# Placement order, weight transposes, index yields and the update of x in a PEER decoder kernel

## The chip, the cores and the metric

One core of a Trainium2 chip runs the whole program in one launch. The metric is the device time of one execution in microseconds; the kernel before has a median of 2251.29 us over 3 runs. The engines are TensorE (PE, with its weight loads shown as PEld), VectorE (DVE), ScalarE (ACT), GpSimd (POOL) and SyncE (SP), which here issues the transfers.

## The reference

A decoder trunk of two layers over 256 tokens of width 1024. In each layer a mixer stage (HGRN2 and stick-breaking attention) is followed by a PEER feed-forward, which is where the change lies:

```python
q = (h @ w_pq).reshape(B, S, 8, 2, 64)
s1, s2 = q[..., 0, :] @ sub_keys[0].T, q[..., 1, :] @ sub_keys[1].T
v1, i1 = lax.top_k(s1, 16); v2, i2 = lax.top_k(s2, 16)
cand = v1[..., :, None] + v2[..., None, :]
top, pos = lax.top_k(cand, 16)
idx = take(i1 * 128 + i2, pos); gates = softmax(top)
act = gelu(einsum(h, peer_u[idx]))
out = einsum(gates * act, peer_v[idx])
```

There are 8 heads, 16384 experts and 256 tokens. After it follows a layer norm of `ALPHA * x + y`, with y scaled by a gate row.

## The kernel before, in words

The kernel doesn't gather experts. It computes all 16384 of them densely, as 128 tiles of 128 experts (`NK`), and multiplies the result by a dense map of gates that is zero where an expert isn't chosen.

**Up stage.** `u_tile` takes a tile j of `peer_u` (128 experts x 1024), turned so that the width lies on partitions and split into a high part and a low part of fp32r, and makes three products with the two parts of h over eight chunks: 24 matmuls of 128x256. Two tiles share a PSUM bank; `fin_u` then applies Gelu on ACT, and multiplies by the gates of the tokens that are already placed (L1618, DVE).

A tile passes through a chain made ahead by `take` and `prep`: transfers from HBM (four on SP's queue), a transpose, a copy that rounds to the high part (ACT, L58), and a subtraction that gives the low part (POOL, L271). Tiles are of two kinds, set by `uv_seq` (L124): kind `u` is turned by one DVE transpose of 128x1024 (`turn`, L220); kind `x`, every fourth tile, by eight PE transposes into PSUM (`prep`, L251), from which ACT copies twice per half, once as the high part and once back into the raw tile. The two kinds are loaded with different layouts. In the down stage a tile j of `peer_v` needs no turning; its low parts come from DVE (L271), and the activations are split by ACT and DVE (`split2`, L521).

**Side work.** Beside the up stage runs a generator, `select`: `topk` finds the candidates and does the index work, and `place_gates` writes the map of gates, in 64 blocks of 4 tokens. `build` compares indices with a ramp on DVE (L1499) and multiplies by the gates (L1504); `prod` makes eight small matmuls of the two into PSUM; `put` brings the result into the map: where tiles are already computed, DVE multiplies them by it (L1531), elsewhere ACT copies it. `pull` deals this work out between tiles: each tile adds a budget to a credit (kept to at most twice the budget), the generator runs on while the credit is above zero, each `yield` takes its number from the credit, and `yield None` ends the turn:

```python
for i, (kind, j) in enumerate(uv_seq[:nu]):
    u_tile(j)
    pull(sides, 1.55 + 1.2 * (kind == "x"))
```

`nu` is 126. What is left of the side work then is drained before PSUM is given to the down stage.

The order on each engine is the order in which the program issues instructions; an engine waits on semaphores for what its operands need.

**Down stage.** The 128 tiles of `peer_v` go into four PSUM banks with 12 matmuls of 128x512 each. Meanwhile the weight and bias rows of the layer norm before are loaded by POOL's queue (`load_row`, issued at step j = 32) into `g_row` and `b_row`, which lie in a buffer whose earlier contents are the gated activations of tiles 12 to 19, and POOL scales and shifts x by them at steps 38 and 44 (lines 1725 to 1728). In layer 1 both rows are loaded again at step 64.

Of the kernel before, what the change touches and what calls it, by code (L numbers as in the profile page):

```python
# [24 lines left out]
NK = 128  # L25
# [16 lines left out]
NB_J = 32  # L42
# [3 lines left out]
def trunk_kernel(ctx: ExitStack, tc: tile.TileContext, x, c, w_ada, b_ada, w_in, lb_logits, hg_norm_g,  # L46
                 w_up_a, w_up_b, w_o, w_pq, sub_keys, peer_u, peer_v, ln_g, ln_b, out):
    nc = tc.nc
# [72 lines left out]
            order.append((kind, w[l][k * P:(k + 1) * P, :], 0))  # L121


    uv_seq = [("x" if j % 4 == 3 else "u", j) for j in range(NK)] + [("v", j) for j in range(NK)]  # L124
    for l in range(DEPTH):
        if l == 0:

# [1191 lines left out]
    def peer(l, hT):  # L1319
        with ExitStack() as es:  # L1320
# [10 lines left out]
            progress = {"j": 0, "t": 0}  # L1331
            with ExitStack() as eu:
# [26 lines left out]
                def topk():  # L1359
# [89 lines left out]
                    for tt in range(2):  # L1449

                        puf = pu[tt].rearrange("p h k -> p (h k)").bitcast(U32)
                        for a in range(2):
                            nc.vector.tensor_scalar(sel[a].bitcast(U32), puf, 4 - 2 * a, None,
                                                    op0=OP.logical_shift_right)
                            nc.vector.tensor_copy(half[2 + a], iu[a][tt].rearrange("p h k -> p (h k)").bitcast(U32))

                        nc.vector.scalar_tensor_tensor(half[0], sel[1].bitcast(U32), -12.0, sel[0].bitcast(U32),
                                                       op0=OP.add, op1=OP.max)
                        for a in range(2):
                            nc.vector.scalar_tensor_tensor(sel[a], half[0], -16.0 + 12 * a, puf, op0=OP.mult, op1=OP.add)  # L1460
                        nc.vector.scalar_tensor_tensor(half[1], sel[1], -48.0, sel[0], op0=OP.add, op1=OP.max)
                        tp = top[tt]
                        yield 0.9
                        for a in range(2):
                            nc.vector.tensor_tensor(m, per_head(half[a])[:, :, :, None].to_broadcast(k4),
                                                    iota_k[:, None, None].to_broadcast(k4), op=OP.is_equal)
                            yield 1.4
                            nc.vector.tensor_mul(m, m, per_head(half[2 + a])[:, :, None].to_broadcast(k4))
                            yield 1.1
                            nc.vector.tensor_reduce(per_head(sel[a]), m, axis=mybir.AxisListType.X, op=OP.add)  # L1470
                            yield 1.4
                        nc.vector.tensor_reduce(sm[:, :PH], tp, axis=mybir.AxisListType.X, op=OP.add)
                        nc.vector.reciprocal(sm[:, :PH], sm[:, :PH])
                        nc.vector.tensor_mul(tp, tp, sm[:, :PH][:, :, None].to_broadcast([P, PH, TOPK]))
                        yield 0.8
                        yield None
                        ptr = psk.tile([P, 512], F32, name="K")
                        for q, src in enumerate((sel[0], sel[1], tp.rearrange("p h k -> p (h k)"))):
                            nc.tensor.transpose(ptr[:, q * P:(q + 1) * P], src, ident)
                        yield None  # L1480
                        nc.vector.tensor_copy(iT[:, tt * P // TB:(tt + 1) * P // TB].rearrange("p b a t -> p a b t"),
                                              ptr[:, :2 * P].rearrange("p (a b t) -> p a b t", a=2, t=TB))

                        nc.vector.tensor_scalar(rest, ptr[:, 2 * P:3 * P], GSCALE, None, op0=OP.mult)
                        pv = rest.rearrange("p (u v) -> p u v", v=2)
                        gp = gT[:, tt * P // 2:(tt + 1) * P // 2]
                        nc.vector.tensor_copy(gp[:, :, 0], pv)
                        nc.vector.tensor_sub(gp[:, :, 1], pv, gp[:, :, 0])
                        yield 0.8
                    yield None  # L1490

                def place_gates():
# [18 lines left out]
                    def prod(b):  # L1511
                        pg = psk.tile([P, TB, NK], F32, name="G")
                        o, og = built.pop(b)
                        for q in range(TB):
                            for a in range(2):
                                mm(pg[:, q], o[:, 0, q // 2, :, q % 2], og[:, q // 2, a, :, q % 2], a == 0, a == 1)
                        return pg

                    def put(b, pg):
# [11 lines left out]
                            nc.vector.tensor_mul(dst, src, dst)  # L1531
                        progress["t"] = (b + 1) * TB

                    built, prods = {}, {}
                    nb = S // TB
                    for b in range(nb + 1):
                        if 0 <= b - 1 < nb:
                            prods[b - 1] = prod(b - 1)
                        if b < nb:
                            build(b)  # L1540
                        yield 1.2
                        if 0 <= b - 1 < nb:
                            put(b - 1, prods.pop(b - 1))

                        yield 0.2 + 0.7 * progress["j"] / NK
                        yield None

                def select():
# [161 lines left out]
                for kind, j in uv_seq[nu:]:  # L1710
                    if kind != "v":
                        u_tile(j)
                        continue
                    state["ahead"] = j < NK - 1
                    delayed.append((j, *take("v"), *wsplit.popleft()))
                    v_prod(0, *delayed[-1])
                    while len(delayed) > max(0, (j - NK + LAST + 1) // 3):
                        v_prod(1, *delayed.popleft())
                    if pend:
                        fin_u(*pend.pop())  # L1720
                    if j == NB_J or l == DEPTH - 1 and j == 2 * NB_J:
                        load_row(g_row, ln_g[l, j // NB_J - 1])
                        load_row(b_row, ln_b[l, j // NB_J - 1])

                    if j in (NB_J + 6, NB_J + 12):
                        xb = from_blocks(xt[j // 6 - (NB_J + 6) // 6])
                        nc.gpsimd.tensor_mul(xb, xb, in_blocks(g_row))
                        nc.gpsimd.tensor_add(xb, xb, in_blocks(b_row))
                    mod_step(mods_left)
                    pull(sides, 0.75)  # L1730
                    if j == NK - 4:
                        drain(sides)
                        row(gt_row, l, GT2, 1.0 / GSCALE)
                        warm_sqrt()
                        if l + 1 < DEPTH:
                            A, B = fold(l, 1, l + 1, SH1, SC1)
                            hT = Modulated()
                            fulls = deque(r[:, i * S:(i + 1) * S] for r in (g_row, b_row) for i in range(4))
# [46 lines left out]
```

## Time and profile before

| | |
|---|---|
| median of 3 runs | 2251.29 us (2247.49 to 2252.64) |
| profiled execution | 2254.38 us |
| its span | 2252.6 us |
| mean granted clock | 0.982 |
| PE busy | 2135.2 us (95%) |
| PE weight loads busy | 1945.4 us (86%) |
| DVE busy | 1817.2 us (81%) |
| ACT busy | 1172.5 us (52%) |
| POOL busy | 1041.5 us (46%) |
| chain that ended last | PE 73%, DVE 16%, DMA 4%, issue 3%, ACT 3% |

All rows are of the profiled execution. A busy PE is not PE at its peak, since matmuls overlap and their ends are modelled; start-to-start distances show its pace. Idle time of an engine matters only where another waits for it. The clock is TensorE's granted clock as a share of full speed.

### The profile page before, as it was taken

Reading aid. Unit: us, or ns where it says so; the run is one execution under the profiler, and the core shown is the slowest. Engines: PE = TensorE matmul, PEld = TensorE weight load, DVE = VectorE, ACT = ScalarE, POOL = GpSimd, SP = SyncE. Lnnn points to the kernel's source line nnn. Section 1 sums busy time; section 2 is a strip of 40 time slices with the busy share of each in tenths; the row PEclk is TensorE's granted clock in tenths of the full one; section 3 lists DMA queues with packets and bytes.
Section 4 is the critical chain, followed back from the end, with each engine's and each line's share of the span. In section 5 each row is a group of like instructions: output and inputs, shape, how many; then the busy total and the mean of one; then the engine's idle time right before and its main releaser. Section 6 shows DMA issues by size and latency. Waiting matters only on the chain.

```text
span 2252.6 us, 42211 instructions
## 1 busy us (share of the span) xinstructions
PE 2135.2 (95%) x14596; PEld 1945.4 (86%) x14596; DVE 1817.2 (81%) x3278; ACT 1172.5 (52%) x2445; POOL 1041.5 (46%) x760
## 2 busy tenths in 40 slices
PE   5789899899999999999989998998999999999998
PEld 5789799899999978888779897997999999788886
DVE  7887989999997488888887558999999955666675
ACT  3446555455555545555545564554555555455562
POOL 4656637787778510000045534577777783200001
PEclk8999999999999999999999999999999999999999
DMA  8646567666667678888844335675766676666662
GB/s 273 196 137 221 159 140 159 129 148 148 142 147 156 176 236 275 281 286 283 298 134 150 113 121 142 147 153 118 154 142 148 146 164 187 202 196 192 193 227 90
DMA packets 498895, 400.32 MB, mean 178 GB/s; under 512 B 291920, under 2 KB 446072, under 8 KB 498680
## 3 DMA queue, kind: packets, MB, share of 16 engines
q1 hardware_dynamic: 496936, 392.33, 62.8%
q0 software_dynamic: 1408, 4.23, 0.6%
q8 instruction: 115, 1.88, 0.3%
q10 hardware_dynamic: 336, 1.06, 0.1%
q14 instruction: 100, 0.82, 0.1%
HBM read 396.46 MB, written 1.05 MB: 176 GB/s over the span
## 4 chain that ended last, share of the span: by engine, by line
PE 73%; DVE 16%; DMA 4%; issue 3%; ACT 3%; POOL 1%; SPq 1%; POOLq 0%; ACTq 0%; DVEq 0%
PE A L61 28%; PE Y L61 27%; PE T L61 7%; PE G L61 4%; PE T L251 2%; DVE wl L271 2%; PE ss L61 2%; PE hs L61 2%; DMA raw<-in_peer_u_dram 2%; POOL wl L271 1%; DVE qk L857 1%; DMA raw<-in_peer_v_dram 1%; DVE raw L220 1%; DVE e L843 1%; DVE o L1504 1%
## 5 line engine op out<-in xcount | busy, mean ns | idle before, releaser
L271 POOL TENSOR_TENSOR wl<-raw,wh 128x512 fp32r<-128x512 f32 x663 | 914.3, 1406 | 700.9 <-ACT wh L58 582.4
L58 ACT ACTIVATE wh<-raw 128x512 fp32r<-128x512 f32 x1060 | 610.8, 623 | 182.0 <-PE A L61 47.6
L61 PE MATMUL A<-hTh,wh 128*128 128x256 f32 x2080 | 543.3, 293 | 11.9 <-ACT wh L58 11.8
L61 PE MATMUL A<-hTl,wh 128*128 128x256 f32 x2080 | 524.2, 284 | 0.0
L61 PE MATMUL Y<-wh,o 128*128 128x512 f32 x1776 | 480.5, 392 | 0.8 <-DVE o L521 0.8
L271 DVE TENSOR_TENSOR wl<-raw,wh 128x512 fp32r<-128x512 f32 x525 | 380.2, 765 | 63.5 <-ACT wh L58 44.9
L61 PEld LDWEIGHTS A<-hTh,wh 128*128 128x128 f32 x2080 | 400.6, 193 | 14.4 <-ACT wh L58 13.7
L61 PEld LDWEIGHTS A<-hTl,wh 128*128 128x128 f32 x2080 | 401.7, 193 | 0.8 <-DVE hTl L521 0.2
L61 PEld LDWEIGHTS Y<-wh,o 128*128 128x128 f32 x1776 | 334.9, 189 | 70.8 <-DVE o L521 1.2
L61 PE MATMUL A<-hTh,wl 128*128 128x256 f32 x2080 | 337.9, 285 | 11.0 <-POOL wl L271 10.9
L61 PEld LDWEIGHTS A<-hTh,wl 128*128 128x128 f32 x2080 | 288.9, 193 | 14.2 <-POOL wl L271 14.2
L61 PE MATMUL Y<-wl,o 128*128 128x512 f32 x888 | 277.9, 393 | 10.4 <-DVE wl L271 10.4
L220 DVE STREAM_TRANSPOSE raw<-raw 128x1024 f32<-128x1024 f32 x192 | 235.1, 1230 | 11.7 <-DMA raw<-in_peer_u_dram 10.1
L58 ACT ACTIVATE o<-buf 128x256 fp32r<-128x256 f32 x228 | 95.1, 417 | 282.7 <-PE Y L61 282.7
L521 DVE TENSOR_TENSOR o<-buf,o 128x256 fp32r<-128x256 f32 x228 | 100.1, 439 | 150.4 <-ACT o L58 150.4
L61 PEld LDWEIGHTS Y<-wl,o 128*128 128x128 f32 x888 | 168.1, 189 | 48.9 <-DVE wl L271 13.8
L1499 DVE TENSOR_TENSOR o<-iT,iota_t 128x1024 f16<-128x1024 f16 x128 | 163.9, 1280 | 0.0
L58 ACT ACTIVATE buf<-G 128x128 f32<-128x128 f32 (+4 forms) x244 | 56.0, 276 | 203.6 <-PE G L61 203.6
L570 POOL TENSOR_TENSOR x<-x,buf 128x1024 f32<-128x1024 f32 x1 | 2.4, 2392 | 291.0 <-DVE x L567 291.0
L61 PE MATMUL T<-hTh,wh 128*128 128x256 f32 x512 | 133.6, 293 | 0.0
L61 PE MATMUL T<-hTl,wh 128*128 128x256 f32 x512 | 130.1, 286 | 0.0
L1504 DVE TENSOR_TENSOR o<-gT,o 128x1024 f16<-128x1024 f16 x128 | 124.6, 973 | 4.4
(496 smaller groups left out, 3254.9 us busy)
## 6 DMA issues: line engine op xcount, KB each, us to landing
raw<-in_peer_u_dram SPq DMA_DIRECT2D x1024, 128.0 KB, 3.5
raw<-in_peer_v_dram SPq DMA_DIRECT2D x256, 512.0 KB, 4.4
raw<-in_w_in_dram SPq DMA_DIRECT2D x88, 512.0 KB, 4.9
raw<-in_w_ada_dram SPq DMA_DIRECT2D x78, 512.0 KB, 4.9
raw<-in_w_o_dram SPq DMA_DIRECT2D x16, 512.0 KB, 3.5
raw<-in_w_pq_dram SPq DMA_DIRECT2D x64, 128.0 KB, 3.4
qk<-in_w_ada_dram SPq DMA_DIRECT2D x10, 512.0 KB, 3.9
e<-in_w_ada_dram SPq DMA_DIRECT2D x8, 512.0 KB, 6.0
```

What stands on the lines that cost most here:

```text
L58: nc.scalar.activation(o, i, f, **kw)
L61: nc.tensor.matmul(o, a, b, start=start, stop=stop, **kw)
L220: nc.vector.transpose(t, t)
L251: nc.tensor.transpose(banks[s][:, q], t[:, (4 * s + q) * P:(4 * s + q + 1) * P], ident)
L271: eng.tensor_sub(lo, src, h.bitcast(F32))
L521: nc.vector.tensor_sub(lo, src, h.bitcast(F32))
L570: nc.gpsimd.tensor_mul(xt[tt], xt[tt], last[0])
L843: eng.tensor_sub(ev[:, :, :hn], mid, bv[:, :, :hn])
L857: nc.vector.tensor_mul(tv[:, :, hn:], nodes(qT, n)[:, :, hn:], ev[:, :, hn:])
L1499: nc.vector.tensor_tensor(o.rearrange("p a u n v -> p (a u) n v"), iT[:, b].rearrange("p a (u v) -> p (a u) v", v=2)[:, :, None] .to_broad ...
L1504: nc.vector.tensor_mul(og.rearrange("p u a n v -> p (u a) n v"), gT[:, b * nu:(b + 1) * nu].rearrange("p u a v -> p (u a) v")[:, :, None] ...
```

## The change

Four edits. Every fourth tile is of kind `x` in the first 64 tiles only; the others from there on become kind `u`, and the budget of their turn falls from 2.75 to 1.55 with the kind. The index work yields after each small instruction, and the charges of the large ones rise. In `place_gates` a turn is now: put block b-2, build block b, issue the matmuls of block b-1 (before: matmuls of b-1, build b, put b-1). And x is scaled and shifted in 16 operations over a quarter of 256 columns, issued at steps 38 to 53, one a step, not in four over 1024.

```diff
-    uv_seq = [("x" if j % 4 == 3 else "u", j) for j in range(NK)] + ...
+    uv_seq = [("x" if j % 4 == 3 and j < NK // 2 else "u", j) for j in range(NK)] + ...
...
                             nc.vector.tensor_scalar(sel[a].bitcast(U32), puf, 4 - 2 * a, None,
                                                     op0=OP.logical_shift_right)
+                            yield 0.5
                             nc.vector.tensor_copy(half[2 + a], iu[a][tt].rearrange("p h k -> p (h k)").bitcast(U32))
+                            yield 0.6
...
                         nc.vector.scalar_tensor_tensor(half[0], sel[1].bitcast(U32), -12.0, sel[0].bitcast(U32),
                                                        op0=OP.add, op1=OP.max)
+                        yield 0.5
                         for a in range(2):
                             nc.vector.scalar_tensor_tensor(sel[a], half[0], -16.0 + 12 * a, puf, op0=OP.mult, op1=OP.add)
+                            yield 0.5
                         nc.vector.scalar_tensor_tensor(half[1], sel[1], -48.0, sel[0], op0=OP.add, op1=OP.max)
                         tp = top[tt]
-                        yield 0.9
+                        yield 0.5
                         for a in range(2):
...
-                            yield 1.4
+                            yield 1.7
                             nc.vector.tensor_mul(m, m, per_head(half[2 + a])[:, :, None].to_broadcast(k4))
                             yield 1.1
                             nc.vector.tensor_reduce(per_head(sel[a]), m, axis=mybir.AxisListType.X, op=OP.add)
-                            yield 1.4
+                            yield 1.6
...
-                    for b in range(nb + 1):
-                        if 0 <= b - 1 < nb:
-                            prods[b - 1] = prod(b - 1)
+                    for b in range(nb + 2):
+                        if b >= 2:
+                            put(b - 2, prods.pop(b - 2))
+
+                            yield 0.2 + 0.7 * progress["j"] / NK
                         if b < nb:
                             build(b)
-                        yield 1.2
-                        if 0 <= b - 1 < nb:
-                            put(b - 1, prods.pop(b - 1))
-
-                        yield 0.2 + 0.7 * progress["j"] / NK
+                            yield 1.2
+                        if 1 <= b <= nb:
+                            prods[b - 1] = prod(b - 1)
                         yield None
...
-                    if j in (NB_J + 6, NB_J + 12):
-                        xb = from_blocks(xt[j // 6 - (NB_J + 6) // 6])
-                        nc.gpsimd.tensor_mul(xb, xb, in_blocks(g_row))
-                        nc.gpsimd.tensor_add(xb, xb, in_blocks(b_row))
+                    n = j - NB_J - 6
+                    if 0 <= n < 16:
+                        xb = from_blocks(xt[n // 8])[:, n % 4]
+                        (nc.gpsimd.tensor_add if n // 4 % 2 else nc.gpsimd.tensor_mul)(
+                            xb, xb, in_blocks(b_row if n // 4 % 2 else g_row)[:, n % 4])
```

## Rows read from the trace of the kernel before

**Rows 1.** the page, busy tenths in 40 slices of 56.3 us, VectorE

```profile
DVE  7887989999997488888887558999999955666675
```

**Rows 2.** busy by stage: stretch, length, PE, PEld, DVE, ACT, POOL (instructions), clock, DMA

```profile
412.00:471.00 59.00, 49.79 (x373) 47.54 (x373) 56.83 (x69) 26.02 (x47) 46.30 (x31) 0.94 0.58 123
471.00:705.00 234.00, 233.22 (x2176) 228.20 (x2175) 229.83 (x335) 129.67 (x342) 180.87 (x129) 1.00 0.66 148
705.00:768.00 63.00, 62.97 (x533) 62.77 (x533) 28.47 (x34) 34.58 (x64) 52.18 (x42) 1.00 0.76 169
1517.00:1576.00 59.00, 47.94 (x356) 45.58 (x355) 57.54 (x67) 25.12 (x45) 41.58 (x29) 0.94 0.58 118
```

**Rows 3.** waits, index stretch 412 to 471 us: total us, times, longest

```profile
PEld A L61 <- POOL wl L271: 7.1, 8, 1.5
```

**Rows 4.** timeline of DVE in the index stretch: start, duration in us

```profile
417.17 0.22 DVE L1453 TENSOR_SCALAR buf<-buf 128x128 uint32<-128x128 uint32 x1
...
420.86 1.23 DVE L220 STREAM_TRANSPOSE raw<-raw 128x1024 f32<-128x1024 f32 x1
```

**Rows 5.** timeline of PE at a tile turned on PE, in the tail

```profile
757.31 0.64 PE L61 MATMUL A<-hTh,wl 128*128 128x256 f32 x4
757.79 1.04 PE L251 MATMUL T<-ident,raw 128*128 128x128 f32 x8
758.58 0.36 PE L61 MATMUL A<-hTh,wh 128*128 128x256 f32 x1
```

**Rows 6.** groups of DVE in the placement stretch, 471 to 705 us

```profile
L1499 DVE TENSOR_TENSOR o<-iT,iota_t 128x1024 f16<-128x1024 f16 x63 | 81.1, 1288 | 0.0
L1504 DVE TENSOR_TENSOR o<-gT,o 128x1024 f16<-128x1024 f16 x63 | 60.7, 963 | 2.2
L220 DVE STREAM_TRANSPOSE raw<-raw 128x1024 f32<-128x1024 f32 x48 | 59.1, 1232 | 0.0
L1531 DVE TENSOR_TENSOR buf<-G,buf 128x128 f32<-128x128 f32 (+19 forms) x129 | 31.9, 289 | 0.0
L1618 DVE TENSOR_TENSOR buf<-A,buf 128x8 f32<-128x8 f32 (+31 forms) x32 | 12.9, 404 | 2.0 <-ACT A L58 1.4
```

**Rows 7.** waits in the placement stretch, 471 to 705 us

```profile
ACT buf L58 <- PE G L61: 99.5, 63, 2.9
...
PEld L61 <- DVE o L1504: 3.6, 14, 0.3
```

**Rows 8.** busy by stage, down stage: x updated in layer 0, undisturbed, layer 1

```profile
826.00:850.00 24.00, 18.38 (x64) 13.95 (x63) 21.43 (x20) 7.96 (x17) 10.46 (x5) 0.86 0.65 215
900.00:925.00 25.00, 25.00 (x114) 20.68 (x113) 21.09 (x36) 12.85 (x27) 0.00 (x0) 1.00 0.84 275
1930.00:1956.00 26.00, 21.26 (x80) 16.44 (x79) 19.34 (x21) 9.74 (x20) 11.59 (x7) 0.87 0.64 202
```

**Rows 9.** timelines of POOL, then DVE, while x is updated in layer 0

```profile
828.91 2.37 POOL L1727 TENSOR_TENSOR x<-x,buf 128x1024 f32<-128x1024 f32 x1
834.82 2.37 POOL L1728 TENSOR_TENSOR x<-x,buf 128x1024 f32<-128x1024 f32 x1 [3.55 <-DMA buf<-in_ln_b_dram]
837.15 2.58 POOL L1727 TENSOR_TENSOR x<-x,buf 128x1024 f32<-128x1024 f32 x1
...
837.40 5.62 DVE L271 TENSOR_TENSOR wl<-raw,wh 128x512 fp32r<-128x512 f32 x2
842.94 0.41 DVE L521 TENSOR_TENSOR o<-buf,o 128x256 fp32r<-128x256 f32 x1
843.28 1.28 DVE L271 TENSOR_TENSOR wl<-raw,wh 128x512 fp32r<-128x512 f32 x2
```

**Rows 10.** instructions of the tile raw: duration ns min/median/max, first and last start

```profile
L271 POOL TENSOR_TENSOR wl<-raw,wh x663: 1260/1302/2957, 19.1 to 1879.6; 128x512 fp32r<-128x512 f32 x166
```

**Rows 11.** instructions of lines 1499 and 1504, the same columns

```profile
L1499 DVE TENSOR_TENSOR o<-iT,iota_t x128: 644/1324/1780, 470.6 to 1811.6; 128x1024 f16<-128x1024 f16 x128
...
L1504 DVE TENSOR_TENSOR o<-gT,o x128: 691/692/1779, 471.3 to 1812.3; 128x1024 f16<-128x1024 f16 x128
```

More of the change, by code (lines that the diff above doesn't have):

```diff
@@ L121, in add_rows @@
             order.append((kind, w[l][k * P:(k + 1) * P, :], 0))
-    uv_seq = [("x" if j % 4 == 3 else "u", j) for j in range(NK)] + [("v", j) for j in range(NK)]
+    uv_seq = [("x" if j % 4 == 3 and j < NK // 2 else "u", j) for j in range(NK)] + [("v", j) for j in range(NK)]
     for l in range(DEPTH):
```

## The prediction, made before the changed kernel was run

> **What bounds the kernel now.** I read the page's slices first: VectorE (DVE) is at nine tenths or more in the 7th to 12th and 26th to 32nd slice, the expert-up stage of the two layers [rows 1]. So the next view is busy time by stage. In layer 0 the up stage falls into three stretches [rows 2]: index work (412 to 471 us), where TensorE (PE) is busy 49.8 of 59 us and its clock averages 0.94; placement (471 to 705), where PE has 233.2 and DVE 229.8 of 234 us, so both are full; and a tail (705 to 768) after the last placement, where PE is full and DVE busy only 28.5 of 63. Layer 1 has the same stretches. Three facts follow. PE loses time in the index work; placement is bound by two engines at once; DVE has some 34 us of air at the end, which comes too late to be used.
>
> The waits in the index stretch say who is late there: weight loads and matmuls wait for the low halves from GpSimd (POOL) [rows 3], which wait for the conversion, which waits for the DVE transpose of a tile. The timeline shows why: seven index operations issued as one lump hold DVE from 417.17 to 420.86, and the tile's transpose starts only then [rows 4].
>
> **Index yields (before lines 1452 to 1471).** Work is dealt out by credit: a tile brings 1.55 (2.75 if its weights are turned on PE), work runs while credit is above zero, each yield charges, and a bare yield ends the turn. Charged per half of the tokens: 0.9 + 2 x 3.9 + 0.8 + 0.8 = 10.3 before, 4.1 + 0.1 + 2 x 4.4 + 1.6 = 14.6 after. At 1.85 a tile on average, two halves take 11 tiles before and 16 after, and with the bare yields 14 and 18 (tiles 26 to 40 and 26 to 44, counting the credit tile by tile). DVE's own work doesn't change: 56.8 busy less 14 x 0.75 transposes of 1.23 [rows 6] is 44 us, and 18 tiles add 18 x 0.75 x 1.23 = 16.6, together 60 us. PE's floor for 18 tiles: 24 matmuls at 0.12 are 2.88 us, a quarter of the tiles adds 0.79 for PE transposes [rows 5], so 3.08 a tile and 55 us. I take 60 us for 18 tiles against 59 for 14: DVE stays the bound, but four more tiles pass below it. Bounds: 55 (PE's floor) to 70 (four tiles more at today's placement pace, nothing won).
>
> **Transposes in the first half only (line 124).** Placement of layer 0 holds 63 blocks and, by 48 DVE and 16 PE transposes, 64 tiles in 234 us: 3.63 us a tile [rows 2, 6]. DVE's groups add up to 245.7 us against 229.8 busy (ends overlap), so I scale by 0.935: a block costs DVE (81.1 + 60.7 + 31.9) x 0.935 / 63 = 2.58 us, a transpose 1.15, the gate product of a tile 0.19 on average and some 0.23 later on. On PE a block costs what is left: (234 - 64 x 2.88 - 16 x 0.79) / 63 = 0.59.
>
> The change takes 16 x 0.79 = 13 us from PE in each layer and puts 16 x 1.15 = 18 us on DVE; the 32 ScalarE copies per layer that go too were on an engine busy 130 of 234 us, and POOL's two subtractions and the four transfers of a tile stay. It also takes 1.2 of credit from each of those 16 tiles. From tile 64 on a tile brings 1.55, a block charges 1.4 + 0.7 j/128, about 1.9, so some 0.85 blocks go to a tile: placement ends at tile 118, not 105, and still ahead of tile 126, so nothing is left to drain with PE idle. Those 54 tiles with 46 blocks cost DVE 46 x 2.58 + 54 x 1.15 + 54 x 0.23 = 193 us, with today's 2% of idle 197; PE needs 54 x 2.88 + 46 x 0.59 = 183. **DVE becomes the bound there**, and 197 is what I take; PE's 183 is the lower bound, the upper one stands under the rivals. The last 8 tiles run at 2.88, 23 us.
>
> **Put ahead of the next comparison (lines 1536 to 1546).** In each turn ScalarE's copies of a block wait for PE's placement matmuls: 99.5 us in 63 waits [rows 7]. Putting block b-2 first makes those waits vanish, as its matmuls were issued a turn earlier. But PE waits for the block's DVE operand only 3.6 us in 234, so there is at most that to win; the block's order on PE's queue stays behind the same tile, and a second block in PSUM has its bank. On DVE the put now stands ahead of the comparison, and both need matmuls of the turn before, so no new wait is queued in front of the transposes. I take nothing, between -3.6 and, if DVE's collisions below shift, a loss priced as the second rival.
>
> **Sum of the up stage**, layer 0, tiles 26 to 126: before 14 tiles in 59, 65 at 3.63 (236), 21 at 3.08 (65), together 360, against 356 in the rows. After: 60 + 20 tiles at 3.6 (72) + 197 + 23 = 352. So -8 by the sums and -4 against the rows; I take -6, and -12 for the two layers.
>
> **x in 16 pieces (lines 1725 to 1728).** Where POOL scales x in the down stage, PE falls: 64 matmuls in 24 us and 80 in 26 at clocks of 0.86 and 0.87, where an undisturbed 25 us has 114 [rows 8]. At 4.56 a microsecond 45 and 39 are missing, 9.9 and 8.5 us, **18 us in all**. The timeline shows the cause: a POOL operation over 128x1024 takes 2.4 us, and two DVE subtractions beside two of these took 5.62 us, not 1.28 [rows 9]: each waited for one POOL operation. The diff spreads the pieces over 16 turns, but that is the order of the program, not of time: the second mul at 837.15 starts right behind the first add, though it is issued six turns (16 us) later than the first mul, and POOL is idle at 900, when nothing of it was left. POOL has nothing else queued, so the pieces will run back to back too, once the rows have landed. A 128x512 operation takes 1.26 [rows 10], one of 1024 2.37; the line through both gives 0.7 for 256 (estimate), 11.3 us for 16 against 10.1 for four. What changes is that DVE gets its turn after 0.7. Layer 1: a step's DVE work is 0.41 + 1.28 = 1.69 us [rows 9], three waits of up to 0.7 make it 3.8 against a step of 2.63 (12 of 114 matmuls in 25 us); 12 pieces in a row last some 3.5 steps and put DVE 4 us behind, of which the tile made one step ahead hides some 2.5. In layer 0 DVE has 21.1 of 25 us, 2.2 a step; with 3.5 waits it is 4.6, and 7 us behind, less 2.5. So 2 and 4 us stay lost, without the fall of the clock, against 9.9 and 8.5: about -12, of which I take **-11**. Bounds: 0 to -18.
>
> The later row loads of layer 1 stand behind the pieces on POOL's queue and start about 1 us later; they are wanted at the end of the span only.
>
> **Together** -12 - 11 = -23 on the profiled execution's 2254.4 us (span 2252.6): 2231. The runs' median stands 3 us below it, so 2229.
>
> **Rivals.**
> *PE's floor.* With ScalarE out of the way and fewer blocks a tile, DVE collides less: its two fp16 operations take 0.64 and 0.69 us undisturbed, 1.29 and 0.96 on average [rows 6, 11]. Then tiles 64 to 118 go at PE's 183 and the index work at 55: 19 us less per layer than above, -23 against the rows for each, with -11 together -57: 2194. For it: 0.9 us a block is waiting; against: POOL is as busy per tile as before. Chance 0.14.
> *DVE's pace worsens.* The same collisions, other way: the new order shifts when the comparison meets POOL's subtractions. Each can wait for a whole one (maxima 1.78 us [rows 11]). From 0.25 us more a block, 46 blocks in each layer give back the 23 us; at 0.45 more it is -23 + 41 = +18, 2269. For it: DVE has no air left before tile 118; against: the mean of both has been the same in both layers. Chance 0.11.
> *Pieces win nothing.* DVE is shut out for 11.3 us in sum, more than before; if PE loses it all, only -12 is left, 2239. Against: PE can draw on a tile made ahead. Chance 0.2. The Trainium skill, SBUF — State Buffer, section "Who interferes with whom", says that a VectorE instruction with two SBUF inputs and a GpSimd instruction that reads SBUF exclude each other for the whole instruction; by that alone cutting an operation up saves no locked time. The trace agrees on the lock with the 5.62 us, but no run here shows pieces.
> *The retuning cancels out.* The extra tiles in the index work only trade places with air, so that the up stage gives its -4 or nothing, and the pieces win little: within 4.5 us. Chance 0.1.
>
> **Numbers.** The forecast (2229, its own range 2212 to 2242) has 0.45. A measurement of this kernel can tell 0.2%, 4.5 us, from no change. Faster: 0.45 + 0.14 + 0.2 = 0.79; same 0.1; slower 0.11. The range leaves out most of the DVE rival and half of PE's floor: 2200 to 2250.
>
> **What would show it.** Last comparison near tile 118, not 105, the tail short; DVE at 98% through it with PE's weight loads waiting for the transpose chain or the block's operand; index stretch PE above 52 of 59 us; no ScalarE wait for the placement matmuls; POOL's 16 pieces within some 20 us, PE there above 90% at full clock. Wrong if L1499 and L1504 change their means by 0.2 us or more, if blocks are drained after tile 126, or if the pieces run one to a step.

## The result, and the profile after

The changed kernel takes 2276.32 us (median of 4 runs, 2276.01 to 2277.69) against 2250.96 for the kernel before: a ratio of 1.0116, 95% interval [1.0098, 1.0133]. That is 25 us slower; 22 us faster had been forecast. Three of the kernels further down (e2, e9 and e12) had one execution each of 11102, 2344 and 5303 us; their medians are those of the other executions. The profiled execution has a span of 2274.6 us, so 22.0 us more than before.

Where these 22.0 us lie shows when both traces are cut at the same events: the first 128x256 matmul of an up stage, the first and the last matmul into Y. The columns are us.

| stage | before | after | difference |
|---|---|---|---|
| up stage, layer 0 | 453.4 | 470.1 | +16.7 |
| down stage, layer 0 | 372.4 | 367.9 | -4.4 |
| mixers, layer 1, and its queries | 277.7 | 278.8 | +1.1 |
| up stage, layer 1 | 456.2 | 470.1 | +13.9 |
| down stage, layer 1, to the end | 369.5 | 363.8 | -5.7 |

The down stages gained 10.2 us, where 11 had been forecast. The up stages were to gain 12 us together and lost 31. Busy time by stage of the changed kernel in layer 0, with the columns of [rows 2]: index work, placement while every fourth tile is turned on PE, placement with all tiles turned on DVE, and the tail:

```profile
412.00:476.00 64.00, 54.98 (x441) 52.71 (x440) 62.93 (x68) 31.04 (x56) 54.08 (x36) 1.00 0.63 136
476.00:550.00 74.00, 72.51 (x670) 70.70 (x669) 69.22 (x98) 40.11 (x104) 60.07 (x41) 1.00 0.68 147
550.00:765.00 215.00, 191.16 (x1681) 181.68 (x1679) 207.91 (x278) 89.34 (x235) 169.05 (x110) 0.99 0.50 135
765.00:787.00 22.00, 22.00 (x188) 22.00 (x186) 14.09 (x19) 11.87 (x22) 20.88 (x17) 1.00 0.72 195
```

The index stretch has 403 matmuls of tiles (the other 38 are transposes), at 24 a tile some 17 tiles in 64 us or 3.8 each, where the kernel before had 14 at 4.1 [rows 2]. The next stretch goes at the old pace. The loss is in the third: 1314 of its 1681 matmuls belong to tiles (the rest are placement), 54.8 tiles in 215 us, **3.93 us a tile where 3.65 was forecast**; PE is busy 191 of 215, and DVE, the bound, 208. DVE's groups of that stretch, as [rows 6]:

```profile
L1508 DVE TENSOR_TENSOR o<-gT,o 128x1024 f16<-128x1024 f16 x46 | 76.7, 1667 | 1.6
L220 DVE STREAM_TRANSPOSE raw<-raw 128x1024 f32<-128x1024 f32 x55 | 67.1, 1227 | 0.0
L1503 DVE TENSOR_TENSOR o<-iT,iota_t 128x1024 f16<-128x1024 f16 x45 | 38.2, 849 | 0.0
```

The transposes cost 1.23 us as ever. The pair of a block, 1503 and 1508 here, 1499 and 1504 before, costs 0.85 + 1.67 = 2.52 us; it was 2.25 in the old placement stretch [rows 6]. Over the whole program each line of the pair (ns, columns as [rows 11]):

```profile
L1503 DVE TENSOR_TENSOR o<-iT,iota_t x128: 644/667/1790, 479.6 to 1879.1; 128x1024 f16<-128x1024 f16 x128
...
L1508 DVE TENSOR_TENSOR o<-gT,o x128: 691/1670/1794, 480.3 to 1879.8; 128x1024 f16<-128x1024 f16 x128
```

The medians have changed places. Before, the comparison usually waited (1324 ns, against a minimum of 644) and the product did not (692); now the comparison is free (667) and the product waits, and waits longer (1670 against 691). Of the 256 operations of the pair 150 take over 1 us in either kernel: not more of them wait, but others, and for longer. One tile of the changed kernel shows why; these are the timelines of DVE, then ACT, POOL and PE, with start and duration in us:

```profile
624.16 1.23 DVE L220 STREAM_TRANSPOSE raw<-raw 128x1024 f32<-128x1024 f32 x1
625.32 0.40 DVE L1623 TENSOR_TENSOR buf<-A,buf 128x272 f32<-128x272 f32 x1
625.65 0.54 DVE L1535 TENSOR_TENSOR buf<-G,buf 128x128 f32<-128x128 f32 x2
626.12 0.67 DVE L1503 TENSOR_TENSOR o<-iT,iota_t 128x1024 f16<-128x1024 f16 x1
626.82 1.67 DVE L1508 TENSOR_TENSOR o<-gT,o 128x1024 f16<-128x1024 f16 x1
...
625.55 1.16 ACT L58 ACTIVATE wh<-raw 128x512 fp32r<-128x512 f32 x2 [1.78 <-POOL wl L271]
...
626.26 3.37 POOL L271 TENSOR_TENSOR wl<-raw,wh 128x512 fp32r<-128x512 f32 x2 [0.87 <-ACT wh L58]
...
628.55 0.63 PE L61 MATMUL G<-o,o 128*128 128x128 f16 x8 [0.70 <-DVE o L1508]
```

The transpose ends at 625.39, and ACT's conversion of that tile starts at 625.55. In this stretch 47 of 53 conversions start within 0.2 us of the end of their transpose; in the placement of the kernel before, 1 of 48. (The profile names POOL's subtraction before as the releaser; it ends in the same moment.) POOL's next subtraction is issued at 626.26, while DVE's comparison runs (626.12 to 626.79). Both have two inputs in SBUF. If they exclude each other, which the experiments on POOL test, POOL gets in when the comparison ends, just ahead of the product, which has to wait for most of it: 1.67 us, not 0.69. PE stands idle 0.70 us for that product before its placement matmuls. The cycle then repeats in the same phase. A tile of the kernel before, DVE, ACT and POOL:

```profile
599.21 1.44 DVE L1499 TENSOR_TENSOR o<-iT,iota_t 128x1024 f16<-128x1024 f16 x1
600.68 0.69 DVE L1504 TENSOR_TENSOR o<-gT,o 128x1024 f16<-128x1024 f16 x1
601.29 0.52 DVE L1531 TENSOR_TENSOR buf<-G,buf 128x128 f32<-128x128 f32 x2
...
599.78 0.41 ACT L58 ACTIVATE buf<-G 128x88 f32<-128x88 f32 x2 [1.95 <-PE G L61]
600.08 1.15 ACT L58 ACTIVATE wh<-raw 128x512 fp32r<-128x512 f32 x2
...
600.80 2.99 POOL L271 TENSOR_TENSOR wl<-raw,wh 128x512 fp32r<-128x512 f32 x2 [0.69 <-ACT wh L58]
```

Here ACT starts with copies that wait 1.95 us for PE's placement matmuls, so the conversion comes at 600.08 and POOL's subtraction at 600.80. The comparison at 599.21 meets the rest of the subtraction before (1.44, not 0.65), and the product at 600.68 gets in ahead of the new one: 0.69. What the copies waited for was free, and it held POOL back.

In the third stretch ACT's copies no longer wait for the placement matmuls (99.5 us in [rows 7]), as forecast, but the wait of PE's weight loads for the product has grown from 3.6 us to 24.6. The waits (total us, times, longest):

```profile
ACT wh L58 <- POOL wl L271: 83.2, 33, 3.7
...
PEld L61 <- DVE o L1508: 24.6, 24, 2.2
...
PE G L61 <- DVE o L1508: 19.8, 24, 2.0
```

In the down stage PE loses less than before while x is updated, at full clock (columns as [rows 8]):

```profile
825.00:850.00 25.00, 22.45 (x99) 18.29 (x98) 20.93 (x29) 12.37 (x26) 3.92 (x6) 1.00 0.87 297
850.00:875.00 25.00, 23.46 (x103) 17.83 (x102) 24.27 (x32) 10.65 (x23) 13.76 (x12) 1.00 0.74 246
```

228 matmuls were due in 50 us at the undisturbed rate, 202 came: 26 missing, 5.7 us, where 45 had been (9.9 us). The pieces do run back to back, four and then twelve, and not one to a step; 13.76 us for twelve is 1.15 us each, as DVE takes turns with POOL there. Beside the four it gets no turn: of two DVE subtractions that take 1.28 us alone, the second starts at 845.78 and ends only after all four, 3.67 us later. That is longer than any beside the four large operations of the kernel before (3.25), and layer 1 shows the same (3.49):

```profile
845.18 4.27 DVE L271 TENSOR_TENSOR wl<-raw,wh 128x512 fp32r<-128x512 f32 x2
...
846.11 2.77 POOL L1734 TENSOR_TENSOR x<-x,buf 128x256 f32<-128x256 f32 x4
851.05 13.76 POOL L1734 TENSOR_TENSOR x<-x,buf 128x256 f32<-128x256 f32 x12 [2.17 <-DMA buf<-in_ln_b_dram]
```

### The profile page after: what moved, and what is told of

It is laid out like the page before. It is cut to its first block, busy times and chain, and to the rows that moved or that the text cites. A ratio compares the mean times of both kernels' runs of the same rounds, so it can differ in the third digit from the quotient of the medians.

```text
span 2274.6 us, 41907 instructions
## 1 busy us (share of the span) xinstructions
PE 2117.0 (93%) x14340; PEld 1917.6 (84%) x14340; DVE 1892.0 (83%) x3324; ACT 1134.0 (50%) x2371; POOL 1098.5 (48%) x784
## 4 chain that ended last, share of the span: by engine, by line
PE 55%; DVE 17%; issue 8%; POOL 8%; DMA 6%; ACT 3%; SPq 2%; POOLq 0%; DVEq 0%; ACTq 0%
PE Y L61 26%; PE A L61 15%; POOL wl L271 8%; PE T L61 6%; DMA raw<-in_peer_u_dram 4%; PE hs L61 2%; PE ss L61 2%; DVE wl L271 2%; PE G L61 2%; SPq L197 2%; DVE o L1508 1%; DVE raw L220 1%; DVE qk L857 1%; PE T L251 1%; DMA raw<-in_peer_v_dram 1%
## 5 line engine op out<-in xcount | busy, mean ns | idle before, releaser
L271 POOL TENSOR_TENSOR wl<-raw,wh 128x512 fp32r<-128x512 f32 x663 | 959.9, 1475 | 675.8 <-ACT wh L58 603.5
L58 ACT ACTIVATE wh<-raw 128x512 fp32r<-128x512 f32 x1124 | 647.6, 622 | 459.3 <-POOL wl L271 241.1
L220 DVE STREAM_TRANSPOSE raw<-raw 128x1024 f32<-128x1024 f32 x224 | 273.6, 1228 | 0.6 <-DMA raw<-in_peer_u_dram 0.5
L1508 DVE TENSOR_TENSOR o<-gT,o 128x1024 f16<-128x1024 f16 x128 | 206.6, 1614 | 4.4
L61 PE MATMUL G<-o,o 128*128 128x128 f16 x1024 | 81.4, 220 | 42.7 <-DVE o L1508 42.7
L1503 DVE TENSOR_TENSOR o<-iT,iota_t 128x1024 f16<-128x1024 f16 x128 | 111.4, 870 | 0.0
```

The source lines that it names most:

```text
L58: nc.scalar.activation(o, i, f, **kw)
L61: nc.tensor.matmul(o, a, b, start=start, stop=stop, **kw)
L220: nc.vector.transpose(t, t)
L271: eng.tensor_sub(lo, src, h.bitcast(F32))
L1503: nc.vector.tensor_tensor(o.rearrange("p a u n v -> p (a u) n v"), iT[:, b].rearrange("p a (u v) -> p (a u) v", v=2)[:, :, None] .to_broad ...
L1508: nc.vector.tensor_mul(og.rearrange("p u a n v -> p (u a) n v"), gT[:, b * nu:(b + 1) * nu].rearrange("p u a v -> p (u a) v")[:, :, None] ...
```

## The experiments

**One edit at a time.** The kernels of the experiments are called e1 to e12. Each of the first four is the kernel before with one of the four edits.

First e1, PE transposes in the first half only:

```diff
-    uv_seq = [("x" if j % 4 == 3 else "u", j) ...
+    uv_seq = [("x" if j % 4 == 3 and j < NK // 2 else "u", j) ...
```

> Kernel before with the PE transposes in the first half only, and nothing else. Theory A (the new order of placement makes the collisions between DVE and POOL; it is not in this kernel): the DVE operations of lines 1499 and 1504 stay near 2.2 us a block together, and the up stage of each layer changes by -4 to +6 us, total within 2243 to 2263. Theory B (the 16 more DVE transposes per layer are the loss by themselves, whatever the order): the up stages are 14 us or more longer each, total about 2280.

Measured: 2253.09 us, ratio 1.0005 [0.9995, 1.0015], no difference. The pair takes 1.11 + 1.17 = 2.28 us a block. Theory B falls: 16 more DVE transposes per layer cost nothing by themselves. That PE gives back as much is likely, not shown.

e2, the order of placement:

```diff
-                        if 0 <= b - 1 < nb:
-                            prods[b - 1] = prod(b - 1)
+                        if b >= 2:
+                            put(b - 2, prods.pop(b - 2))
...
                             build(b)
...
-                            put(b - 1, prods.pop(b - 1))
+                            prods[b - 1] = prod(b - 1)
```

> Kernel before with put ahead of the next comparison, and nothing else. Theory A (the order makes the collisions): L1504 (its line here) takes about 1.6 us on average where it took 0.96, the pair some 0.3 us a block more, about +15 us per layer, total about 2275 or more. Theory C (the collisions need both, the order and tiles that are all turned on DVE): the pair stays within 0.1 us of the kernel before, total within 2246 to 2256.

Measured: 2290.38 us, ratio 1.0185 [1.0164, 1.0205]: **some 40 us slower, more than the whole change**. The up stages are 18.6 and 17.3 us longer. The pair, over the whole program:

```profile
L1504 DVE TENSOR_TENSOR o<-gT,o 128x1024 f16<-128x1024 f16 x128 | 184.4, 1441 | 4.4
L1499 DVE TENSOR_TENSOR o<-iT,iota_t 128x1024 f16<-128x1024 f16 x128 | 123.3, 963 | 0.0
```

2.40 us a block against 2.25 in the kernel before (1.280 + 0.973 over its whole program): theory A, not C. The 0.15 us are 10 us over 64 blocks, though, of 18 lost. DVE also idles more: in the placement stretch its gate product (L1618, here 1619) waits 7.8 us for ACT's Gelu, 1.4 before [rows 6].

e3, the index yields:

```diff
                             nc.vector.tensor_scalar(sel[a].bitcast(U32), puf, ...
+                            yield 0.5
...
-                            yield 1.4
+                            yield 1.7
```

> Kernel before with the index yields only. By the prediction's step: four more tiles pass beside the index work for 1 to 5 us more, the tail is shorter by five tiles: -4 to -9 us per layer, total 2235 to 2245. Rival: DVE is the bound from the topk work on, so the tiles only trade places: within 2247 to 2256.

Measured: 2244.20 us, ratio 0.9972 [0.9961, 0.9982]: 7 us faster, up stages 3.7 and 5.3 us shorter. The gain is real and at the small end. The down stage of layer 0, which the edit doesn't touch, is 3.9 us shorter in that trace too.

e4, x in 16 pieces:

```diff
-                    if j in (NB_J + 6, NB_J + 12):
-                        xb = from_blocks(xt[...])
-                        nc.gpsimd.tensor_mul(xb, ...); nc.gpsimd.tensor_add(xb, ...)
+                    n = j - NB_J - 6
+                    if 0 <= n < 16:
+                        xb = from_blocks(xt[n // 8])[:, n % 4]
+                        (nc.gpsimd.tensor_add if n // 4 % 2 else nc.gpsimd.tensor_mul)(xb, xb, ...)
```

> Kernel before with x in 16 pieces only. The changed kernel's down stages were 4.4 and 5.8 us shorter than those of the kernel before: if that is the pieces alone, this kernel takes about 2241 (2238 to 2244). Rival: the down stage is shorter because of something that the other edits leave behind (a tile of peer_v made earlier), then within 2248 to 2254.

Measured: 2246.18 us, ratio 0.9975 [0.9962, 0.9988], 5 us faster (3 to 9 by the interval), between the two ranges expected. In its trace the down stages are 5.5 and 5.9 us shorter, so the pieces do it by themselves; the up stages of that one execution are 2.6 and 1.3 us longer than those of before, which the edit doesn't touch. How much is scatter shows in all fourteen traces. In layer 1 the down stage takes 368.0 to 369.5 us without the pieces and 363.7 to 363.9 with them, a plain gain of 5 us; in layer 0 it takes 368.4 to 373.1 without and 365.4 to 369.1 with them, 3 us by the means. Together that is 8 us.

**What of the order is slow.** In the next kernel, e5, put is cut in two: put itself makes ACT's copies, right behind the matmuls again, and hands back DVE's products, which stay ahead of the comparison of the following turn.

```diff
                         if b >= 2:
-                            put(b - 2, prods.pop(b - 2))
+                            for dst, src in prods.pop(b - 2):
+                                nc.vector.tensor_mul(dst, src, dst)
...
                         if 1 <= b <= nb:
-                            prods[b - 1] = prod(b - 1)
+                            prods[b - 1] = put(b - 1, prod(b - 1))
```

> The kernel of e2 (put ahead of the comparison), but put is cut in two: ScalarE's copies of block b-1 are issued right behind its matmuls, as in the kernel before, and only DVE's product of block b-2 stands ahead of the comparison. Theory A1 (ScalarE's wait for the placement matmuls, which e2 lost, kept the conversion and with it POOL's subtraction behind the end of a tile on PE, out of the way of line 1504): the pair of lines 1499 and 1504 is back at 2.2 to 2.3 us, total 2246 to 2260. Theory A2 (the place of DVE's product between the transpose and the comparison is what shifts the pair into POOL's subtraction): as slow as e2, 2280 or more.

Measured: 2270.37 us, ratio 1.0095 [1.0071, 1.0118]: between the two, so neither theory as it stands. The pair is back at 1.22 + 1.07 = 2.29 us, as A1 has it, and up to 640 us the trace of layer 0 goes at the old pace. Later it doesn't; stretches of 20 us, the columns of [rows 2]:

```profile
600.00:620.00 20.00, 19.97 (x187) 19.59 (x186) 19.36 (x29) 11.12 (x30) 15.79 (x12) 1.00 0.60 145
660.00:680.00 20.00, 18.09 (x169) 17.48 (x169) 18.82 (x24) 10.01 (x28) 14.36 (x11) 1.00 0.53 128
```

At 600 us PE is full and DVE has 19.4 of 20; at 660 PE has 18.1 and DVE 18.8, DVE waiting for Gelu and then PE for DVE. Up to 640 us none of 34 conversions starts within 0.2 us of its transpose, and the product takes over 1 us in 13 of 46 blocks; after that 6 of 15 do, and the product takes over 1 us in 11 of 17. So the product's wait comes with the early conversion, as A1 has it. That the place of DVE's product is needed too is shown by e9 below. Why conversions come early again at the end, and what else makes this kernel 20 us slower with the pair at 2.29 us, was not settled.

**Is it POOL?** Both orders (e6 the old one, e7 the new one), with POOL's subtraction of the up stage replaced by an operation that reads nothing. The low part of the weights is left out there.

```diff
-            eng.tensor_sub(lo, src, h.bitcast(F32))
+            if kind in "ux":
+                nc.gpsimd.memset(lo.bitcast(F32), 0.0)
+            else:
+                eng.tensor_sub(lo, src, h.bitcast(F32))
```

> Kernel before, with POOL's subtraction for the tiles of peer_u replaced by a memset of the low half to zero (the low part of the weights is left out of the up stage; the products are still made with it). POOL then reads nothing there. If the pair of lines 1499 and 1504 is slowed by POOL's two-input operations alone, it falls to 1.34 us (0.65 + 0.69), and DVE gets some 0.9 us a block back; total some 8 to 25 us below the kernel before, PE being the next bound.

> The kernel of e2 with the same memset in place of POOL's subtraction (low part of the weights left out in the up stage). Theory A (the new order is slow because of collisions with POOL): the 40 us between e2 and the kernel before shrink to under 8 between this kernel and e6. Rival (the order is slow by its waits among DVE, ScalarE and PE, whatever POOL does): 20 us or more are left.

Measured: 2214.55 us with the old order, ratio 0.9841 [0.9819, 0.9863], and 2213.72 with the new one, 0.9837 [0.9815, 0.986]. **The 40 us between the orders are gone**, and all four up stages take 435.8 us. The gain, 36 us, is larger than expected. The pair of the old order:

```profile
L1507 DVE TENSOR_TENSOR o<-gT,o 128x1024 f16<-128x1024 f16 x128 | 88.6, 692 | 4.4
L1502 DVE TENSOR_TENSOR o<-iT,iota_t 128x1024 f16<-128x1024 f16 x128 | 86.2, 674 | 0.0
```

and of the new one:

```profile
L1507 DVE TENSOR_TENSOR o<-gT,o 128x1024 f16<-128x1024 f16 x128 | 88.6, 692 | 4.4
L1502 DVE TENSOR_TENSOR o<-iT,iota_t 128x1024 f16<-128x1024 f16 x128 | 86.6, 677 | 0.0
```

0.69 + 0.68 us, within 0.03 us of the minima of [rows 11], although POOL writes just as much:

```profile
L272 POOL MEMSET wl<- 128x512 f32 x512 | 269.5, 526 | 615.3 <-PE A L61 590.9 <-PE G L61 20.7 <-PE K L1482 3.7
```

The Trainium skill, SBUF — State Buffer, section "Who interferes with whom", says that a VectorE instruction with two SBUF inputs contends with a GpSimd instruction that reads SBUF and not with one that only writes it; these runs agree.

The size of the gain is not that of the collisions of the pair. A memset is also shorter (0.53 us against 1.41 on average), and of the 17.6 and 20.4 us by which e6's up stages are shorter, 15.6 and 18.5 lie ahead of the first comparison. From the first comparison to the last it gains 2.7 and 2.6 us only, since PE was full there before (19.9 of each 20 us). What gains is the index stretch, without any index yields; its row, beside 49.79 us of PE and a clock of 0.94 in [rows 2]:

```profile
412.00:471.00 59.00, 58.68 (x504) 58.28 (x502) 51.20 (x65) 33.99 (x66) 19.33 (x37) 1.00 0.75 162
```

That the orders come out equal shows that the loss needs POOL's subtraction. By itself it doesn't show the collisions: DVE is busy only 14 to 17 of each 20 us in these placements, so that other waits of DVE would cost nothing either.

**Shorter operations on POOL.** POOL's subtraction of the up stage in operations of 256 columns (part holds half i of the three operands), once on e2's kernel (e12) and once on e8's, the best version so far (e11; e8 stands below).

```diff
-            eng.tensor_sub(lo, src, h.bitcast(F32))
+            if kind in "ux":
+                for i in range(2):
+                    nc.gpsimd.tensor_sub(*part)
```

> The kernel of e2 (put ahead of the comparison alone) with the same cut of POOL's subtraction. Theory A: the waits halve here too, of e2's 40 us 15 or more are won back, total under 2276. Rival: 2285 or more.

Measured: 2252.16 us, ratio 1.0002 [0.9992, 1.0012]: 38 us of e2's loss are won back without touching the order. Of the 41 us between the two traces 25 lie in the placements and 9 ahead of them. The pair, and POOL's operation:

```profile
L1512 DVE TENSOR_TENSOR o<-gT,o 128x1024 f16<-128x1024 f16 x128 | 142.1, 1110 | 4.4
L1507 DVE TENSOR_TENSOR o<-iT,iota_t 128x1024 f16<-128x1024 f16 x128 | 120.1, 939 | 0.0
```

```profile
L277 POOL TENSOR_TENSOR wl<-raw,wh 128x256 fp32r<-128x256 f32 x1024 | 850.6, 868 | 80.9 <-ACT wh L58 35.8 <-issue 18.8 <-POOL wl L277 14.4
```

The product now waits 0.42 us, in all 128 blocks (1.10 to 1.12 us), not 0.75 as on average in e2 (1.441 - 0.691) or 0.98 in the changed kernel's median.

> The kernel of e8 with POOL's subtraction of the up stage cut into operations of 256 columns. Theory A (a DVE operation waits for the POOL operation that runs, so half the length is half the wait): the pair of lines 1503 and 1508 falls from 2.25 to some 1.8 to 2.0 us, total 2222 to 2232. Rival (DVE loses as much as POOL works, in however many pieces): pair within 0.1 us of 2.25, total 2233 or more by POOL's further starts.

Measured: 2234.44 us, ratio 0.9923 [0.9907, 0.994], the same as the uncut kernel below. The pair falls about as expected, from 2.25 to 2.01 us, but the time is the rival's. Nothing comes of the shorter pair: PE was full in e8's placement already (19.9 of each 20 us), and now POOL is full too, which had some 15.5 of 20 there (columns of [rows 2]):

```profile
560.00:580.00 20.00, 19.97 (x190) 19.49 (x188) 18.55 (x29) 10.72 (x30) 20.00 (x23) 1.00 0.68 146
```

**Combinations.** First the two edits that gain, then the changed kernel without one of the other two.

e8, the kernel before with the index yields and the pieces, so with both of these diffs:

```diff
+                            yield 0.5
...
+                    if 0 <= n < 16:
+                        xb = from_blocks(xt[n // 8])[:, n % 4]
```

> Kernel before with the index yields and the 16 pieces, old order of placement, PE transposes throughout. If the two gains add: 7.3 + 5.3 = 12.6 us below the kernel before, 2239 (2235 to 2243). If they share a cause, 2243 to 2246.

Measured: 2235.22 us, ratio 0.9932 [0.9915, 0.9949], 15 us faster: the gains add. **This version beats both kernels**, and the one with POOL's subtraction cut as well (2234.44) ties with it.

e9, the changed kernel with the order of before:

```diff
-                        if b >= 2:
-                            put(b - 2, prods.pop(b - 2))
+                        if 0 <= b - 1 < nb:
+                            prods[b - 1] = prod(b - 1)
...
-                            prods[b - 1] = prod(b - 1)
+                            put(b - 1, prods.pop(b - 1))
```

> The changed kernel with the old order of placement (half, index yields and pieces stay). If the order is the only loss and the rest adds up as it was measured one by one: near e8, 2235 to 2240, since e1 showed the half as worth nothing. Rival (the later end of placement after the index yields makes the half a loss): 2245 or more. Rival (with the tail's air gone into the index work the half is a gain): under 2232.

Measured: 2246.46 us, ratio 0.9978 [0.9965, 0.999]. Without the order the change would have been a small gain, 5 us; but beside the index yields the half is a loss, 11 us against e8. Index work and the last placement stretch of this kernel:

```profile
412.00:476.00 64.00, 56.05 (x441) 54.10 (x440) 62.97 (x66) 31.52 (x57) 54.09 (x35) 0.97 0.63 135
550.00:745.00 195.00, 181.31 (x1640) 175.08 (x1638) 188.78 (x270) 90.65 (x231) 161.31 (x106) 1.00 0.51 144
```

Of 1640 matmuls 1280 are tiles': 53.3 in 195 us, 3.66 each.

This kernel also tells what of the order shifts the pair. In that stretch 41 of 53 conversions start within 0.2 us of their transpose, nearly as in the changed kernel, and yet the pair takes only 2.22 us. A tile, DVE, ACT and POOL:

```profile
616.52 1.23 DVE L220 STREAM_TRANSPOSE raw<-raw 128x1024 f32<-128x1024 f32 x1
617.68 0.64 DVE L1503 TENSOR_TENSOR o<-iT,iota_t 128x1024 f16<-128x1024 f16 x1
618.35 0.69 DVE L1508 TENSOR_TENSOR o<-gT,o 128x1024 f16<-128x1024 f16 x1
...
617.83 1.15 ACT L58 ACTIVATE wh<-raw 128x512 fp32r<-128x512 f32 x2 [0.58 <-DVE raw L220]
...
618.54 1.66 POOL L271 TENSOR_TENSOR wl<-raw,wh 128x512 fp32r<-128x512 f32 x1 [1.26 <-ACT wh L58]
```

The comparison follows the transpose at once, so the product already runs when POOL's subtraction is issued at 618.54, and neither operation of the pair waits. So it is in all 17 blocks with an early conversion and nothing between transpose and comparison. In the other 16 with an early conversion the gate product of a tile stands between them, and in all 16 the product takes over 1 us. In the changed kernel put's own product always stands there. The shift thus needs both halves of the new order: ACT's early conversion, and DVE's product ahead of the comparison.

e10, the changed kernel with PE transposes throughout:

```diff
-    uv_seq = [("x" if j % 4 == 3 and j < NK // 2 else "u", j) ...
+    uv_seq = [("x" if j % 4 == 3 else "u", j) ...
```

> The changed kernel with PE transposes throughout (new order, index yields, pieces). If the parts add: e2's 40 less 13 to 15, 2274 to 2280, the same as the changed kernel. If the collisions of the new order need tiles that are all turned on DVE, under 2265.

Measured: 2271.35 us, ratio 1.0084 [1.0067, 1.0101]. That lies between the two expectations. With the order in, the half costs only 5 us more (2276.32); the collisions don't need it.

**Side by side.** The pace of placement in layer 0, from the start of the first comparison to that of the last, in us a tile, and the pair over the whole program:

| kernel | order | us a tile | pair, us |
|---|---|---|---|
| before | old | 3.64 | 2.25 |
| e1, half | old | 3.66 | 2.28 |
| e8, index, pieces | old | 3.62 | 2.25 |
| e9, half, index, pieces | old | 3.66 | 2.29 |
| e2 | new | 3.89 | 2.40 |
| e10, index, pieces | new | 3.91 | 2.38 |
| changed kernel | new | 3.86 | 2.48 |
| e5, ACT's copies as before | in part new | 3.76 | 2.29 |
| e6 and e7, POOL reads nothing | old and new | 3.59 and 3.59 | 1.37 and 1.37 |
| e11 and e12, POOL's operation halved | old and new | 3.64 and 3.67 | 2.01 and 2.05 |

The new order costs 0.20 to 0.30 us a tile, 0.03 with POOL's operation halved and nothing where POOL reads nothing.

## Why the prediction was wrong

The up stages were forecast to gain 12 us and lost 31. Of these 43 us some 30 lie between e9 and the changed kernel, which differ in the order alone; the other 13 are there in e9 too, whose up stages take as long as before.

**The order of placement** is the step that failed. It was costed at nothing, "between -3.6 and, if DVE's collisions below shift, a loss priced as the second rival". It cost some 40 us alone and 30 inside the change (e9 to the changed kernel). The sum asked what waits for the block's operand and found 3.6 us; it saw that 99.5 us of ACT's waiting would vanish, and did not ask what ACT would start earlier. ACT starts the conversion, and so POOL's subtraction, as soon as the transpose is done; and with DVE's product between transpose and comparison, the subtraction falls between the comparison and the product of the pair. e9 shows that both are needed for the shift (17 blocks against 16). That the loss needs POOL's subtraction is shown by e6 and e7, that it hangs on the length of that operation by e12. The pair's rise over e9, from 2.29 to 2.48 us, is 12.5 us of the 15 that each up stage loses. In e2 it is 10 of 18; that the rest is DVE's idle time, waiting for Gelu, is not shown.

**The rival "DVE's pace worsens"** is what came, and its mechanism, that "the new order shifts when the comparison meets POOL's subtractions", is the one found. Its price was near: 0.25 us more on 46 blocks of a layer are 11.5 us, 0.20 on all 64 were 12.5. Its chance of 0.11 looks low: the reason given against it, that both layers showed the same mean, was no evidence, as both run the same order. The medians of [rows 11] would have told more: 1324 of at least 644 on one line and 692 of at least 691 on the next is not chance meeting but a phase, which an edit that moves either neighbour can shift. A shift alone isn't a loss, though: in e9 the product's median is 1643 and the pair takes 2.29 us.

**The index yields** were mis-sized. 60 us for 18 tiles was forecast; the changed kernel takes 64 for 17, and e9's stretch is the same. That is 68 for 18, so of the gain of some 13 us (four more tiles in nearly the same time) 4 to 5 a layer are left, as e3's up stages show (3.7 and 5.3). (The forecast's upper bound, four tiles at the pace of placement, is 59 + 4 x 3.63 = 73.5 and not 70.) The clock did hold, 1.00 and 0.97 against 0.94, and DVE was the bound as forecast, but PE still waits 6.6 us for the low half, 5.4 before. The prediction laid that wait on the lump of index operations on DVE (eight in the trace, not seven). e6 has the same lump and no such wait, and PE is busy 58.7 of 59 us: what held the tiles up was POOL's subtraction. Whether by its length or by collisions with the index work is open.

**Transposes in the first half only**: the pace was right where the order is the old one. 3.65 us a tile was forecast, e9 shows 3.66; the last comparison came at tile 118 as counted from the credits, and nothing was drained. (The old pace of 3.63 is 234 us over 64.5 tiles; the 64 named with it give 3.66.) By the prediction's own sums the second half costs more than before (197 + 23 against 214), and only the index gain was to pay for it. With that gain at a third, the up stages of e9 are 455.0 and 455.3 us, as before: the two cancel.

**The pieces**: near in size, and right in mechanism in part. -11 was forecast; the down stages gained 10.2 us in the changed kernel and 11.3 in e4, some 8 by all traces, and e4's median 5.3. They run back to back and the clock no longer falls, as forecast. But DVE gets its turn after 0.7 us beside twelve of the sixteen only; beside the first four it waits for all of them.

**PE's floor** as a rival was priced at -23 a layer and needed the collisions gone. With the memset they are, on the kernel before, and placement gains 2.7 us a layer, as PE was full already; the rest of the 18 to 20 us comes from the index stretch. With tiles turned on DVE alone it was not tried.

## What to carry to other kernels

An engine's wait may be what keeps two others apart: before removing it, follow what the engine will start earlier and what that meets. Where two instructions contend, read minimum, median and maximum of each line, not the mean: a median at the floor on one and far above it on the next is a phase, and any reordering near it can change the price and should get a wide range. A background operation in short pieces made such an order nearly harmless here; where PE was the bound already (e11), they won nothing.

## What the runs showed of the hardware

A DVE operation with two SBUF inputs that follows another such one at once can wait for most of a POOL operation that gets in between: the product took 1.67 us by the median, against 0.69 alone, and over 1 us in 120 of the changed kernel's 128 blocks; with POOL's operation halved (e12) it took 1.10 to 1.12 us in all 128. It is not always turn about: one DVE subtraction waited through four POOL operations in a row, 3.67 us.

Sixteen POOL operations of 256 columns (0.69 us each in a row, 1.15 in turns with DVE) in place of four of 2.4 to 2.7 us cost PE 5.7 us in layer 0 and not 9.9. POOL's work on them grew from 10.0 to 16.5 us and the longest wait of DVE didn't fall; the granted clock was 1.00, not 0.86. A subtraction of 256 columns took 0.87 us in e12, more than half of the 1.41 for 512 in the kernel before, and POOL was busy 20.0 of each 20 us through most of e12's placement.
